# A two-layer hybrid decoder on one core: two weight fetches of layer 0's MLP moved ahead, its down groups reordered, and fewer down units threaded into the up

## The chip, the cores and the metric

The kernel runs on one core of a Trainium2 chip. The metric is the device time of one execution in microseconds (us), and of several executions the median. The engines are PE (TensorE, the matrix products), DVE (VectorE), ACT (ScalarE), POOL (GpSimd) and SP (SyncE, which here issues most DMAs); each works through its own instructions in order, and semaphores tie them together.

## The reference

All is float32, one sequence of 512 tokens, width 1024, MLP width 2816:

```python
def forward(x):
    h = x
    for i in range(2):
        hn = rms_norm(h, norm_mix[i])
        h = h + (pool_mixer(hn) if i == 0 else swa_sink_attention(hn))
        hn = rms_norm(h, norm_ffn[i])
        u = hn @ w_in                       # 1024 -> 2 * 2816
        c = causal_depthwise_conv3(u) + conv_b
        a, g = c[..., :2816], c[..., 2816:]
        h = h + (a * silu(g)) @ w_out       # 2816 -> 1024
    return rms_norm(h, norm_f)
```

The pool mixer takes causal means over windows of 2, 4, 8 and 16 tokens in four channel groups; the attention is a sliding window of 128 with 16 query heads, 4 key heads, sinks and ALiBi.

## The kernel before, in words

Activations lie with channels on the 128 partitions and tokens along the free axis; `h` is eight such tiles of 128 x 512. Every float32 product is made of three matmuls of rounded parts: each operand is split into a high part (`_h`, an ACT copy, line 101 or 427) and the rest (`_l`, a subtraction on DVE or POOL, line 104 or 428), and `mm3` (lines 87 to 89) issues high x high, high x low and low x high.

The change lies in layer 0's MLP, `mlp_halves`. The MLP width is cut into 22 blocks of 128 (j = 0 to 21), each with a gate part and a value part.

- **Blocks 0 to 6** are done as 14 plain chunks (gate and value, eight `mm3` each). Their weights are `wi`; the `_l` part of these is made on POOL in four pieces. After each chunk a short text in the table of line 537 says, by the chunk's number, which other steps are issued: `1` takes one finished chunk through norm, convolution and gating (a "late job" on DVE and ACT), `0` and `2` build the activation sums `th`/`tl`, `f` fetches a block's summed weights, `r` and `v` split them, `m` fetches and splits the first down weights.
- **Blocks 7 to 21** are each done with seven half-size products in place of eight, on sums of quarters of the weights and sums of token halves. A block has four weight tiles: `uw_u` (two sums, made by a plain DMA on SP and an accumulating DMA on POOL into the same tile), `uw_r` (two plain quarters), `uw_v` (made from `uw_r` and `uw_u` by two adds on POOL, in place in the `uw_r` tile, lines 450 and 451) and `uw_q` (one quarter). A product is twelve matmuls of 256 columns. In an iteration j of the loop the next block's weights are split (`first_weights`, `second_weights`) and those of the block after that fetched (`fetch_sums`).
- **The down product** of layer 0 runs inside this loop. Finished blocks `z` are taken in groups (`DOWN0` gives their sizes); for each group and each of the eight tiles of `h` (m = 0 to 7) one down weight `wo` is fetched, split and used: a group of four has four *units* per m, a unit being one `mm3` of 512 columns. `FILL` gives how many units an iteration j threads between its products, at four stops; what remains runs behind the loop. The last group also makes, for each m, the normalised input of the attention (`ax`, lines 240 and 241) and its square sums (lines 204 and 213).

Buffers come from rings: `wh`/`wl` of 4 serve `uw_r`, `uw_q`, `wi` and `wo` together; `vh`/`vl` of 3 serve `uw_u` and `uw_v`; `raw` of 3 holds fetched weights; `sq` of 2 holds a fetched down weight and also the squares. The finished blocks z4 to z18 lie in the ring of eight that also holds other activations, the first four and the last three in their own.

The order of instructions on each engine is set by a list scheduler: it takes the steps as the program writes them, with its own costs, and puts each engine's instructions in one order, which the chip then follows.

Of the kernel before, what the change touches and what calls it, by code (L numbers as in the profile page):

```python
# [19 lines left out]
F32 = mybir.dt.float32  # L20
F32R = mybir.dt.float32r
# [13 lines left out]
FF = 2816  # L35
NF = FF // P
GROUPS = ((4, True), (4, True), (3, False))
DOWN0 = (4, 4, 4, 4, 4, 2)
PLAIN = 7
SETS = ((2, 2), (2, 2))  # L40
HD = 64
# [19 lines left out]
def trunk(ctx: ExitStack, tc: tile.TileContext, x_tok, x_t, vecs, w_pool, w_kq, w_v, w_o, gain, w_in, w_half, w_down, w_end, w_tok, out):  # L61
# [18 lines left out]
    def bank(tag):  # L80
        rings[tag].append(rings[tag].pop(0))
        return banks[rings[tag][-1]]
# [13 lines left out]
    def weights(src, n, name, eng=None, raw=None, step=1024, pin=lambda ins: ins):  # L96

        raw = raw or fetch(src, n, name)
        h = wp.tile([P, 1024], F32R, tag="wh", name=f"{name}_h")
        l = wp.tile([P, 1024], F32R, tag="wl", name=f"{name}_l")  # L100
        pin(A.activation(h[:, :n], raw[:, :n], AF.Copy))  # L101
        for a in range(0, n, step):
            o = slice(a, min(a + step, n))
            (eng or V).tensor_tensor(l[:, o], raw[:, o], h[:, o].bitcast(F32), ALU.subtract)  # L104
        return h, l
# [253 lines left out]
    def mlp_halves(fp, xs, norm, ws0, after):  # L359
# [9 lines left out]
        def valued(j, ps):  # L369
            t = conv_sum(fp, ps, j, f"a{j}")  # L370
            V.tensor_tensor(t, t, gate.pop(j), ALU.mult)
            own = j < 4 or j >= NF - 3
            zh, zl = (
                fp.tile([P, S], F32R, tag=f"z{k}", name=f"z{j}{k}", bufs=4)
                if own
                else xp.tile([P, S], F32R, tag=f"x{k}", name=f"z{j}{k}")
                for k in "hl"
            )
            A.activation(zh, t, AF.Copy)
            V.tensor_tensor(zl, t, zh.bitcast(F32), ALU.subtract)  # L380
            z.append((zh, zl))
# [8 lines left out]
        def blocks(t):  # L390
            return t.rearrange("p (a b) -> p a b", a=2)
# [33 lines left out]
        def own_split(raw, name):  # L425
            x, y = (fp.tile([P, 1024], F32R, tag=f"v{k}", name=f"{name}_{k}", bufs=3) for k in "hl")
            A.activation(x, raw, AF.Copy)  # L427
            V.tensor_tensor(y, raw, x.bitcast(F32), ALU.subtract)  # L428
            return x, y

        raws, uw = {}, {}

        def fetch_sums(j):

            src = w_half[j - PLAIN]
            u = fp.tile([P, 1024], F32, tag="ur", name=f"uw{j}_u_raw", bufs=2)
            nc.sync.dma_start(blocks(u), src[:, 0:4:2, :])
            pin(G.dma_start(blocks(u), src[:, 2:4, :], accum_op=ALU.add))
            r = wp.tile([P, 1024], F32, tag="raw", name=f"uw{j}_r_raw", bufs=3)
            nc.sync.dma_start(blocks(r), src[:, 0:2, :])  # L440
            raws[j] = u, r

        def first_weights(j):

            n = 4 * P
            u, r = raws[j]
            q = wp.tile([P, 1024], F32, tag="raw", name=f"uw{j}_q_raw", bufs=3)
            nc.sync.dma_start(q[:, :n], w_half[j - PLAIN][:, 3, :])
            R = weights(None, 2 * n, f"uw{j}_r", raw=r)
            G.tensor_tensor(r[:, :n], r[:, :n], u[:, n:], ALU.add)  # L450
            G.tensor_tensor(r[:, n:], r[:, n:], r[:, :n], ALU.add)
            raws[j] = r, q
            uw[j] = R, own_split(u, f"uw{j}_u")

        def second_weights(j):

            r, q = raws.pop(j)
            uw[j] += own_split(r, f"uw{j}_v"), weights(None, 4 * P, f"uw{j}_q", raw=q)

        def product(out, w, b, t, start=True):  # L460
            for p in range(4):
# [66 lines left out]
        for at in range(2, len(todo)):  # L528
            w, ps, ahead = ahead, chunk(at), load(at + 1)
            for k in range(NC):  # L530
                if at == 3 and k == 0:
                    r = norm.stats(bank("aux"), root=True)
                if at == 3 and k == 5:
                    rb = norm.spread(bank("aux"), r)
                    signs = spread_signs()
                mm3(ps, part(w, k), xs[k], k == 0, k == NC - 1)
            for x in {3: "00", 4: "00", 5: "1", 6: "22", 7: "12", 8: "21", 9: "1f1", 10: "1", 11: "1r", 12: "1vf", 13: "1m1"}.get(at, ""):
                if x == "0":
                    first_part(len(th))
                elif x == "2":  # L540
                    second_part(len(tv))
                elif x == "1":
                    work()
                elif x == "f":
                    fetch_sums(PLAIN + fetched)
                    fetched += 1
                elif x == "r":
                    first_weights(PLAIN)
                elif x == "m":
                    down_fetch(0)  # L550
                    down_fetch(1)
                    down_split(0)
                else:
                    second_weights(PLAIN)

        FILL = dict(zip(range(PLAIN, NF), (11, 11, 10, 11, 11, 10, 8, 8, 8, 8, 8, 8, 8, 8, 8)))
        fills = down()

        def fill(j, i):
# [8 lines left out]
        for j in range(PLAIN, NF):  # L568
            R, U, W, Q = uw.pop(j)
            if j + 1 < NF:  # L570
                first_weights(j + 1)
            ba, bx = bank("ps"), bank("ps")
            s1, s2 = (fp.tile([P, HS], F32, tag="sn", name=f"sn{j}{i}", bufs=4) for i in range(2))
            s3 = sm.tile([P, S], F32, tag="sqa", name=f"sn{j}2", bufs=1)[:, lo]

            product(ba[:, lo], R, 0, 0)
            A.activation(s1, ba[:, lo], AF.Copy)  # L577
            if last:
                last()
            work()  # L580
            fill(j, 0)
            product(ba[:, lo], W, 0, 5, False)
            A.activation(s2, ba[:, lo], AF.Copy, scale=-1.0)
            if j + 1 < NF:
                second_weights(j + 1)
            if j + 2 < NF:
                fetch_sums(j + 2)
            product(bx[:, lo], R, 1, 1)
            fill(j, 1)
            work()  # L590
            product(ba[:, lo], U, 0, 3, False)
            A.activation(s3, ba[:, lo], AF.Copy)
            product(bx[:, hi], U, 1, 4)
            fill(j, 2)
            product(ba[:, lo], Q, 0, 6, False)
            V.tensor_tensor(ba[:, hi], bx[:, hi], s3, ALU.add)
            jobs.append((gated, j, ba))
            work()

            def last(j=j, bx=bx, W=W, s1=s1, s2=s2):  # L600
                product(bx[:, hi], W, 1, 2, False)
                V.tensor_tensor(bx[:, lo], bx[:, lo], s1, ALU.subtract)
                V.tensor_tensor(bx[:, hi], s2, bx[:, hi], ALU.subtract)
                jobs.append((valued, j, bx))

            fill(j, 3)
# [644 lines left out]
```

## Time and profile before

| what | us |
|---|---|
| median of three runs | 938.29 (937.98 to 939.18) |
| the profiled execution | 939.86 |
| its span, first to last instruction | 938.2 |
| PE busy | 902.0 (96%) |
| DVE busy | 702.8 (75%) |
| ACT busy | 482.4 (51%) |
| POOL busy | 248.8 (27%) |
| mean granted PE clock, of full speed | 0.981 |

Matmuls are pipelined, so the duration of one is longer than the distance to the next. In a row of the time line stand the start, the duration, the engine, the line of the program, the operation, output<-inputs with buffer numbers left out, the shape, and in brackets the idle time of the engine before it with what ended it. "PE bank L87 <- ACT wo_h L101" in the list of waits reads: the matmul of line 87 waited for the ACT copy of line 101 that makes `wo_h`.

### The profile page before, as it was taken

To read this page: it belongs to the slowest core of one execution; us is meant where nothing else is said; L and a number is where in the kernel's file an instruction comes from. 1 tells how busy PE (TensorE), PEld (TensorE's weight loads), DVE (VectorE), ACT (ScalarE), POOL (GpSimd) and SP (SyncE) were. 2 spreads that over 40 slices of the span, in tenths; PEclk is the share of its full clock that TensorE was granted. 3 is DMA by queue.
4 is the path that set the end of the run, shared out by engine and by line. 5 is a ranking of instruction groups with operands and counts; after the bars stand their busy time and mean duration, and the time that the engine had idled before them with its cause. 6 is when DMAs were issued, how large, how long until landed. Compare 5 with 4: busy or idle time off the path is not lost.

```text
span 938.2 us, 13044 instructions
## 1 busy us (share of the span) xinstructions
PE 902.0 (96%) x4812; PEld 774.6 (83%) x4812; DVE 702.8 (75%) x1116; ACT 482.4 (51%) x776; POOL 248.8 (27%) x319
## 2 busy tenths in 40 slices
PE   8999679999999999879999999999999999999996
PEld 8888469999999999649888988888888888888885
DVE  7899587868787876655688664498896788976744
ACT  7755345545555654344788643365443444443434
POOL 3856311312323220150766322000230001210004
PEclk9999869999999999989999999999999999999999
DMA  8433335555555533122211013316268322443302
GB/s 326 139 112 80 101 105 152 136 148 143 148 156 148 156 104 97 37 101 68 92 45 47 23 64 138 112 46 221 71 161 246 110 90 68 90 138 110 103 32 90
DMA packets 37120, 106.85 MB, mean 114 GB/s; under 512 B 3904, under 2 KB 4928, under 8 KB 37056
## 3 DMA queue, kind: packets, MB, share of 16 engines
q1 hardware_dynamic: 33744, 93.95, 30.3%
q0 software_dynamic: 3312, 12.06, 7.4%
q8 instruction: 38, 0.62, 0.3%
q14 instruction: 26, 0.21, 0.1%
HBM read 103.90 MB, written 2.10 MB: 113 GB/s over the span
## 4 chain that ended last, share of the span: by engine, by line
PE 84%; DVE 5%; ACT 4%; POOL 2%; issue 2%; DMA 2%; DVEq 0%; ACTq 0%; POOLq 0%
PE bank L87 27%; PE bank L89 27%; PE bank L88 26%; DMA uw_u_raw<-w_half 2%; POOL wi_l L104 2%; PE bank L1083 1%; PE bank L1111 1%; DVE n_acc L502 1%; PE bank L285 1%; ACT sc L1099 0%; ACT wi_h L101 0%; ACT px_h L240 0%; ACT h L329 0%; DMA xt<-x_tok 0%; PE bank L726 0%
## 5 line engine op out<-in xcount | busy, mean ns | idle before, releaser
L87 PE MATMUL bank<-f1x_h,wi_h 128*128 128x512 f32 x352 | 137.9, 392 | 0.0
L89 PE MATMUL bank<-f1x_h,wi_l 128*128 128x512 f32 x352 | 137.1, 389 | 0.0
L88 PE MATMUL bank<-f1x_l,wi_h 128*128 128x512 f32 x352 | 137.0, 389 | 0.0
L101 ACT ACTIVATE wi_h<-wi_raw 128x1024 fp32r<-128x1024 f32 x58 | 61.3, 1060 | 88.7 <-PE bank L88 72.6
L89 PEld LDWEIGHTS bank<-f1x_h,wi_l 128*128 128x128 f32 x352 | 66.1, 188 | 13.9
L88 PEld LDWEIGHTS bank<-f1x_l,wi_h 128*128 128x128 f32 x352 | 66.1, 188 | 13.6
L87 PEld LDWEIGHTS bank<-f1x_h,wi_h 128*128 128x128 f32 x352 | 66.1, 188 | 13.4
L104 DVE TENSOR_TENSOR wi_l<-wi_raw,wi_h 128x1024 fp32r<-128x1024 f32 x44 | 53.7, 1225 | 30.2 <-ACT wi_h L101 29.4
L450 POOL TENSOR_TENSOR uw_r_raw<-uw_r_raw,uw_u_raw 128x512 f32<-128x512 f32 x15 | 20.0, 1336 | 187.6 <-DVE uw_r_l L104 182.0
L101 ACT ACTIVATE wo_h<-wo_raw 128x512 fp32r<-128x512 f32 (+2 forms) x56 | 36.9, 660 | 57.5 <-PE bank L88 55.7
L104 POOL TENSOR_TENSOR wi_l<-wi_raw,wi_h 128x256 fp32r<-128x256 f32 x56 | 55.0, 1014 | 34.3 <-ACT wi_h L101 34.3
L615 DVE TENSOR_TENSOR c_u<-bank,n_rb 128x512 f32<-128x512 f32 x44 | 30.1, 687 | 23.3 <-PE bank L89 23.3
L89 PE MATMUL bank<-f0x_h,wi_l 128*128 128x512 f32 x112 | 43.7, 390 | 1.0 <-POOL wi_l L104 1.0
L213 POOL TENSOR_TENSOR n_acc<-n_acc,n_sq 128x512 f32<-128x512 f32 x14 | 20.7, 1479 | 89.6 <-DVE h L492 47.1
L88 PE MATMUL bank<-f0x_l,wi_h 128*128 128x512 f32 x112 | 43.6, 389 | 0.0
L87 PE MATMUL bank<-f0x_h,wi_h 128*128 128x512 f32 x112 | 43.2, 391 | 0.0
L492 DVE TENSOR_TENSOR h<-bank,h 128x512 f32<-128x512 f32 x48 | 32.9, 685 | 12.8 <-PE bank L89 12.5
L620 DVE SCALAR_TENSOR_TENSOR c_t<-c_u,vec,c_t 128x510 f32<-128x510 f32 x44 | 40.9, 932 | 1.2
L104 DVE TENSOR_TENSOR wo_l<-wo_raw,wo_h 128x512 fp32r<-128x512 f32 (+2 forms) x52 | 36.6, 704 | 4.0 <-ACT wo_h L101 2.6
L87 PE MATMUL bank<-th,uw_v_h 128*128 128x256 f32 x120 | 34.6, 288 | 4.2 <-ACT sn L577 4.2
L757 POOL TENSOR_TENSOR wt_a_raw<-wt_a_raw,wt_s_raw 128x1024 f32<-128x1024 f32 x4 | 11.3, 2836 | 101.6 <-DVE wt_a_l L104 101.6
L428 DVE TENSOR_TENSOR uw_v_l<-uw_r_raw,uw_v_h 128x1024 fp32r<-128x1024 f32 x15 | 18.5, 1232 | 25.3 <-ACT uw_v_h L427 25.3
(438 smaller groups left out, 2858.8 us busy)
## 6 DMA issues: line engine op xcount, KB each, us to landing
wi_raw<-w_in SPq DMA_DIRECT2D x58, 512.0 KB, 3.4
wo_raw<-w_down SPq DMA_DIRECT2D x40, 256.0 KB, 3.4
uw_u_raw<-w_half SPq DMA_DIRECT2D x15, 512.0 KB, 3.7
uw_r_raw<-w_half SPq DMA_DIRECT2D x15, 512.0 KB, 4.0
uw_u_raw<-w_half POOLq DMA_DIRECT2D x15, 512.0 KB, 6.5
wt_a_raw<-w_tok SPq DMA_DIRECT2D x12, 512.0 KB, 4.7
kq_raw<-w_kq SPq DMA_DIRECT2D x10, 512.0 KB, 3.3
wo_raw<-w_o SPq DMA_DIRECT2D x8, 512.0 KB, 3.3
```

The costliest lines, as they stand in the source:

```text
L87: T.matmul(ps, lhsT=wh, rhs=xh, start=start, stop=False, **kw)
L88: T.matmul(ps, lhsT=wh, rhs=xl, start=False, stop=False, **kw)
L89: T.matmul(ps, lhsT=wl, rhs=xh, start=False, stop=stop, **kw)
L101: pin(A.activation(h[:, :n], raw[:, :n], AF.Copy))
L104: (eng or V).tensor_tensor(l[:, o], raw[:, o], h[:, o].bitcast(F32), ALU.subtract)
L213: eng.tensor_tensor(self.acc[:, lo:hi], self.acc[:, lo:hi], sq[:, lo:hi], ALU.add)
L428: V.tensor_tensor(y, raw, x.bitcast(F32), ALU.subtract)
L450: G.tensor_tensor(r[:, :n], r[:, :n], u[:, n:], ALU.add)
L492: V.tensor_tensor(h[m], ps, h[m], ALU.add)
L615: V.tensor_tensor(u, ps, rb, ALU.mult)
L620: V.scalar_tensor_tensor(t[:, 2:], u[:, : S - 2], cw[0], t[:, 2:], ALU.mult, ALU.add)
L757: G.tensor_tensor(r[:, :n], r[:, :n], raws["s1", s][:, :n], ALU.add)
```

## The change

Five edits, all in `mlp_halves` and its constants:

1. The summed weights of blocks 7 and 8 (`fetch_sums`) are fetched together after chunk 8 (`ff`), in place of one after chunk 9 and one after chunk 12. The plain quarters `uw_r`, which were fetched in the same step, are a step of their own (`fetch_rows`, `g`), after chunk 9 and chunk 13.
2. Block 7's `uw_r` and `uw_q` go to other tiles: one of the `vl` ring and one of the `sq` ring in place of two of the `raw` ring.
3. POOL's two adds for `uw_v` are a step of their own (`add_weights`, `a`), after chunk 12 for block 7. One more late job is issued after the chunks (eleven in place of ten).
4. The down groups have 4, 4, 2, 4, 4, 4 blocks in place of 4, 4, 4, 4, 4, 2; the last four finished blocks get tiles of their own.
5. `FILL`: from block 10 on, 9, 8, 8 and then 7 units an iteration in place of 11, 11, 10 and then 8. In all 120 in place of 136; 56 in place of 40 run behind the loop.

```diff
@@ -35,7 +35,7 @@
 FF = 2816
 NF = FF // P
 GROUPS = ((4, True), (4, True), (3, False))
-DOWN0 = (4, 4, 4, 4, 4, 2)
+DOWN0 = (4, 4, 2, 4, 4, 4)
 PLAIN = 7
 SETS = ((2, 2), (2, 2))
 HD = 64
@@ -369,7 +369,7 @@
         def valued(j, ps):
             t = conv_sum(fp, ps, j, f"a{j}")
             V.tensor_tensor(t, t, gate.pop(j), ALU.mult)
-            own = j < 4 or j >= NF - 3
+            own = j < 4 or j >= NF - 4
             zh, zl = (
                 fp.tile([P, S], F32R, tag=f"z{k}", name=f"z{j}{k}", bufs=4)
                 if own
@@ -430,32 +430,45 @@

         raws, uw = {}, {}

+        us, rs = {}, {}
+
         def fetch_sums(j):

             src = w_half[j - PLAIN]
-            u = fp.tile([P, 1024], F32, tag="ur", name=f"uw{j}_u_raw", bufs=2)
+            u = us[j] = fp.tile([P, 1024], F32, tag="ur", name=f"uw{j}_u_raw", bufs=2)
             nc.sync.dma_start(blocks(u), src[:, 0:4:2, :])
             pin(G.dma_start(blocks(u), src[:, 2:4, :], accum_op=ALU.add))
-            r = wp.tile([P, 1024], F32, tag="raw", name=f"uw{j}_r_raw", bufs=3)
-            nc.sync.dma_start(blocks(r), src[:, 0:2, :])
-            raws[j] = u, r
+
+        def fetch_rows(j):
+
+            if j > PLAIN:
+                rs[j] = wp.tile([P, 1024], F32, tag="raw", name=f"uw{j}_r_raw", bufs=3)
+            else:
+                rs[j] = fp.tile([P, 1024], F32R, tag="vl", name=f"uw{j}_r_raw", bufs=3).bitcast(F32)
+            nc.sync.dma_start(blocks(rs[j]), w_half[j - PLAIN][:, 0:2, :])

         def first_weights(j):

             n = 4 * P
-            u, r = raws[j]
-            q = wp.tile([P, 1024], F32, tag="raw", name=f"uw{j}_q_raw", bufs=3)
+            u, r = us[j], rs[j]
+            if j > PLAIN:
+                q = wp.tile([P, 1024], F32, tag="raw", name=f"uw{j}_q_raw", bufs=3)
+            else:
+                q = sm.tile([P, S], F32, tag="sq", name=f"uw{j}_q_raw")
             nc.sync.dma_start(q[:, :n], w_half[j - PLAIN][:, 3, :])
-            R = weights(None, 2 * n, f"uw{j}_r", raw=r)
+            raws[j] = q
+            uw[j] = weights(None, 2 * n, f"uw{j}_r", raw=r), own_split(u, f"uw{j}_u")
+
+        def add_weights(j):
+
+            n = 4 * P
+            u, r = us.pop(j), rs[j]
             G.tensor_tensor(r[:, :n], r[:, :n], u[:, n:], ALU.add)
             G.tensor_tensor(r[:, n:], r[:, n:], r[:, :n], ALU.add)
-            raws[j] = r, q
-            uw[j] = R, own_split(u, f"uw{j}_u")

         def second_weights(j):

-            r, q = raws.pop(j)
-            uw[j] += own_split(r, f"uw{j}_v"), weights(None, 4 * P, f"uw{j}_q", raw=q)
+            uw[j] += own_split(rs.pop(j), f"uw{j}_v"), weights(None, 4 * P, f"uw{j}_q", raw=raws.pop(j))

         def product(out, w, b, t, start=True):
             for p in range(4):
@@ -534,7 +547,7 @@
                     rb = norm.spread(bank("aux"), r)
                     signs = spread_signs()
                 mm3(ps, part(w, k), xs[k], k == 0, k == NC - 1)
-            for x in {3: "00", 4: "00", 5: "1", 6: "22", 7: "12", 8: "21", 9: "1f1", 10: "1", 11: "1r", 12: "1vf", 13: "1m1"}.get(at, ""):
+            for x in {3: "00", 4: "00", 5: "1", 6: "22", 7: "12", 8: "21ff", 9: "1g1", 10: "1r", 11: "11", 12: "1av", 13: "g1m1"}.get(at, ""):
                 if x == "0":
                     first_part(len(th))
                 elif x == "2":
@@ -546,6 +559,10 @@
                     fetched += 1
                 elif x == "r":
                     first_weights(PLAIN)
+                elif x == "g":
+                    fetch_rows(PLAIN + (at > 12))
+                elif x == "a":
+                    add_weights(PLAIN)
                 elif x == "m":
                     down_fetch(0)
                     down_fetch(1)
@@ -553,7 +570,7 @@
                 else:
                     second_weights(PLAIN)

-        FILL = dict(zip(range(PLAIN, NF), (11, 11, 10, 11, 11, 10, 8, 8, 8, 8, 8, 8, 8, 8, 8)))
+        FILL = dict(zip(range(PLAIN, NF), (11, 11, 10, 9, 8, 8, 7, 7, 7, 7, 7, 7, 7, 7, 7)))
         fills = down()

         def fill(j, i):
@@ -569,6 +586,7 @@
             R, U, W, Q = uw.pop(j)
             if j + 1 < NF:
                 first_weights(j + 1)
+                add_weights(j + 1)
             ba, bx = bank("ps"), bank("ps")
             s1, s2 = (fp.tile([P, HS], F32, tag="sn", name=f"sn{j}{i}", bufs=4) for i in range(2))
             s3 = sm.tile([P, S], F32, tag="sqa", name=f"sn{j}2", bufs=1)[:, lo]
@@ -585,6 +603,7 @@
                 second_weights(j + 1)
             if j + 2 < NF:
                 fetch_sums(j + 2)
+                fetch_rows(j + 2)
             product(bx[:, lo], R, 1, 1)
             fill(j, 1)
             work()
```

POOL's order around the accumulating fetches. Before, with `wi0_5_1` the weights of chunk 10, and so on:

```order
L104 TENSOR_TENSOR wi0_4_0_l_811<-wi0_4_0_raw_808,wi0_4_0_h_810 128x256 x4
L104 TENSOR_TENSOR wi0_5_1_l_857<-wi0_5_1_raw_854,wi0_5_1_h_856 128x256 x4
L438 DMA uw7_u_raw_897<-w_half 128x1024
L104 TENSOR_TENSOR wi0_5_0_l_911<-wi0_5_0_raw_908,wi0_5_0_h_910 128x256 x4
L104 TENSOR_TENSOR wi0_6_1_l_954<-wi0_6_1_raw_951,wi0_6_1_h_953 128x256 x4
L450 TENSOR_TENSOR uw7_r_raw_900<-uw7_r_raw_900,uw7_u_raw_897 128x512
L451 TENSOR_TENSOR uw7_r_raw_900<-uw7_r_raw_900 128x512
L104 TENSOR_TENSOR wi0_6_0_l_1005<-wi0_6_0_raw_1002,wi0_6_0_h_1004 128x256 x4
L438 DMA uw8_u_raw_1053<-w_half 128x1024
```

And in the changed program:

```order
L104 TENSOR_TENSOR wi0_4_0_l_811<-wi0_4_0_raw_808,wi0_4_0_h_810 128x256 x4
L440 DMA uw7_u_raw_854<-w_half 128x1024
L440 DMA uw8_u_raw_857<-w_half 128x1024
L104 TENSOR_TENSOR wi0_5_1_l_863<-wi0_5_1_raw_860,wi0_5_1_h_862 128x256 x4
L104 TENSOR_TENSOR wi0_5_0_l_914<-wi0_5_0_raw_911,wi0_5_0_h_913 128x256 x4
L466 TENSOR_TENSOR uw7_r_raw_903<-uw7_r_raw_903,uw7_u_raw_854 128x512
L467 TENSOR_TENSOR uw7_r_raw_903<-uw7_r_raw_903 128x512
L104 TENSOR_TENSOR wi0_6_1_l_967<-wi0_6_1_raw_964,wi0_6_1_h_966 128x256 x4
L104 TENSOR_TENSOR wi0_6_0_l_1016<-wi0_6_0_raw_1013,wi0_6_0_h_1015 128x256 x4
```

Both accumulating fetches moved ahead of the splits of chunks 10 to 13, and the two adds for block 7 ahead of those of chunks 12 and 13. The plain DMAs into the same two tiles stand on SP at the same place in both programs, ahead of block 5's weights.

ACT's order where block 8's summed weights are split. Before:

```order
L427 ACTIVATE uw7_v_h_1045<-uw7_r_raw_900 128x1024
L354 ACTIVATE g4_t_1083<-bank2_72,vec_90 128x512
L379 ACTIVATE z3h_1041<-a3_t_1036 128x512
L427 ACTIVATE uw8_u_h_1114<-uw8_u_raw_1053 128x1024
L101 ACTIVATE uw7_q_h_1049<-uw7_q_raw_990 128x512
L354 ACTIVATE a4_t_1097<-bank3_73,vec_90 128x512
L367 ACTIVATE g4_t_1083<-g4_t_1083 128x512
L101 ACTIVATE wo0_0_h_1092<-wo0_0_raw_1088 128x512
```

In the changed program it stands before the last two plain chunks' weights:

```order
L427 ACTIVATE uw7_v_h_1054<-uw7_r_raw_903 128x1024
L427 ACTIVATE uw8_u_h_1118<-uw8_u_raw_857 128x1024
L367 ACTIVATE g2_t_906<-g2_t_906 128x512
L101 ACTIVATE wi0_6_1_h_966<-wi0_6_1_raw_964 128x1024
L379 ACTIVATE z2h_950<-a2_t_945 128x512
L354 ACTIVATE g3_t_998<-bank6_76,vec_90 128x512
L354 ACTIVATE a3_t_1004<-bank7_77,vec_90 128x512
L101 ACTIVATE wi0_6_0_h_1015<-wi0_6_0_raw_1013 128x1024
```

What stood behind it before (`uw7_q`, block 4's value part, the first down weight `wo0_0`) now follows the same late work without it.

In the up, ACT's order at the end of iteration 11 in the changed program, and PE's at the same place (`wo1_4` is the down weight of group 1, m = 4):

```order
L427 ACTIVATE uw12_v_h_1912<-uw12_r_raw_1750 128x1024
L101 ACTIVATE wo1_4_h_1944<-wo1_4_raw_1840 128x512
L101 ACTIVATE wo1_5_h_2006<-wo1_5_raw_1948 128x512
L354 ACTIVATE g11_t_1994<-bank4_74,vec_90 128x512
L595 ACTIVATE sn120_2024<-bank0_70 128x256
```

```order
L87 MATMUL bank4_74<-th3_665,uw11_q_h_1743 128x256
L88 MATMUL bank4_74<-tl3_666,uw11_q_h_1743 128x256
L89 MATMUL bank4_74<-th3_665,uw11_q_l_1744 128x256
L87 MATMUL bank3_73<-z7h_1408,wo1_3_h_1836 128x512
L88 MATMUL bank3_73<-z7l_1409,wo1_3_h_1836 128x512
L89 MATMUL bank3_73<-z7h_1408,wo1_3_l_1837 128x512
L87 MATMUL bank2_72<-z4h_1094,wo1_4_h_1944 128x512
L88 MATMUL bank2_72<-z4l_1095,wo1_4_h_1944 128x512
L87 MATMUL bank0_70<-th0_611,uw12_r_h_1844 128x256
L88 MATMUL bank0_70<-tl0_612,uw12_r_h_1844 128x256
L89 MATMUL bank2_72<-z4h_1094,wo1_4_l_1945 128x512
```

The down weight's split follows that of `uw12_v` on ACT, and PE uses it one unit behind the Q product of iteration 11. Where a new down weight begins in an iteration follows from `FILL` and `DOWN0`, so with 7 units it drifts from one iteration to the next; with 8 units and groups of four it was at the same two stops in each.

## The prediction

> **What bounds the kernel now.** I read the page's busy shares first, then what PE waited for, then the stages by windows, then the time line of the two stages in which PE stops.
>
> ```profile
> span 938.2 us, 13044 instructions
> PE 902.0 (96%) x4812; PEld 774.6 (83%) x4812; DVE 702.8 (75%) x1116; ACT 482.4 (51%) x776; POOL 248.8 (27%) x319
> ...
> PE bank L87 <- ACT wo_h L101: 12.4, 4, 8.4
> PE bank L87 <- ACT sn L577: 4.2, 1, 4.2
> PE bank L89 <- DVE wo_l L104: 3.5, 4, 2.1
> PE bank L89 <- POOL wi_l L104: 1.0, 1, 1.0
> ```
>
> PE sets the time, at 96%, so only what makes PE wait, or run at a lower clock, can be won. The waits are few: in total us, number of times, longest. The windows (PE, PEld, DVE, ACT, POOL busy; then the granted clock) say where they lie.
>
> ```profile
> 90.00:100.00 10.00, 10.00 (x46) 8.28 (x45) 10.00 (x15) 5.95 (x9) 4.30 (x3) 1.00 0.16 52
> ...
> 110.00:120.00 10.00, 1.22 (x2) 0.50 (x2) 4.62 (x7) 3.99 (x7) 0.00 (x0) 0.55 0.44 112
> 120.00:130.00 10.00, 5.33 (x19) 4.42 (x20) 9.74 (x15) 5.47 (x11) 3.28 (x3) 0.50 0.13 33
> 130.00:140.00 10.00, 10.00 (x64) 9.23 (x64) 6.14 (x10) 4.48 (x8) 0.46 (x1) 0.93 0.58 151
> 142.00:363.00 221.00, 221.00 (x1504) 204.74 (x1504) 174.86 (x237) 119.97 (x179) 52.88 (x38) 1.00 0.51 141
> 363.00:414.00 51.00, 41.67 (x189) 32.07 (x188) 32.02 (x52) 22.23 (x38) 13.10 (x26) 0.94 0.14 43
> ```
>
> Two holes: 110 to 131, where the clock also stands at one half (0.55, 0.50, then 0.93), and one after 363, with 9 us of PE missing. Between them, from 142 to 363, PE never stops and has the full clock: the change can only lose there.
>
> **The first hole**, in the time line:
>
> ```profile
> 76.81 1.03 POOL L438 DMA_DIRECT2D uw_u_raw<-w_half  x1
> ...
> 101.27 4.24 POOL L104 TENSOR_TENSOR wi_l<-wi_raw,wi_h 128x256 fp32r<-128x256 f32 x4
> 105.46 0.89 POOL L438 DMA_DIRECT2D uw_u_raw<-w_half  x1
> 108.36 0.28 PE L88 MATMUL bank<-tl,uw_r_h 128*128 128x256 f32 x1
> 108.48 0.28 PE L89 MATMUL bank<-th,uw_r_l 128*128 128x256 f32 x1
> 113.77 1.06 ACT L427 ACTIVATE uw_u_h<-uw_u_raw 128x1024 fp32r<-128x1024 f32 x1 [8.20 <-DMA uw_u_raw<-w_half]
> 115.38 0.69 DVE L104 TENSOR_TENSOR uw_q_l<-uw_q_raw,uw_q_h 128x512 fp32r<-128x512 f32 x1 [7.95 <-ACT uw_q_h L101]
> 117.11 0.80 PE L87 MATMUL bank<-z0h,wo_h 128*128 128x512 f32 x1 [8.35 <-ACT wo_h L101]
> 126.32 0.37 ACT L577 ACTIVATE sn<-bank 128x256 f32<-128x256 f32 x1
> 126.74 0.58 PE L87 MATMUL bank<-th,uw_v_h 128*128 128x256 f32 x1 [4.22 <-ACT sn L577]
> ```
>
> POOL issues the accumulating fetch of block 8's summed weights at 105.46, because four splits stand ahead of it in its queue. The data is there at 113.7. ACT stands before that tile's split for 8.20 us, and behind it in ACT's order are uw7_q, the late chunks and the first down weight; so DVE stops for 7.95 us and PE for 8.35. Then DVE is the limit: from 115.38 to 126 it works without a gap (9.74 of 10 in the window), and ACT copies the first bank (line 577) only at 126.32, behind that work. PE's waits there add to 8.35 + 2.1 (the longest for wo_l above) + 4.2 = 14.7 us.
>
> **Part A: the early fetch.** In the new order both accumulating fetches stand on POOL before block 5's splits. Their plain halves are issued on SP long before in both programs, so only POOL's place held them. The wait of ACT is gone if the transfer takes its usual time:
>
> ```profile
> uw_u_raw<-w_half POOLq DMA_DIRECT2D x15, 512.0 KB, 6.5
> ```
>
> That is 6.5 us at the median, 8.3 here. Block 7's own fetch was issued at 76.81, right behind block 5's first four splits; both now stand ahead of these, so before 76.81. Even one behind the other at 8.3 us each, the second is there by 93.4, and its split stands at 113.77 today. What then? DVE's work in the stretch is the same: the late chunks (one job fewer is left for the loop), the splits, z4 and z5. So I do not count the whole hole. Everything behind DVE's pause comes 7.95 us earlier: line 577 at 118.4 and PE's second start at 118.8 in place of 126.74. The wait for the first down weight shrinks to one or two us, the wait for line 577 stays at about 5. **A = -8.0 us.** Ends: -4 if half of the work merely stays ahead of line 577 (DVE has no pause then, but uw8_u's split and one more chunk now stand in the chunks' time), -10.5 if the clock does not fall, which is worth about 2.5 us (30 matmuls at about twice 0.12 to 0.23).
>
> On that last point the rows come first: PE's last matmul starts at 108.48, and 0.55 in the window to 120 means 1 us at full clock and 9 at half, so the clock fell at about 111, 2.2 us after PE stopped, and came back near 131.4. The Trainium skill ("TensorE: Matmul & The Clock Gate", Part 1: The HAM clock gate) says that the clock is halved after an idle window of about 3.4 us that runs free of the program. By it a pause of 5 us may or may not hold a whole window, and A would be -8 or -10.5; the trace of this case shows a shorter pause punished.
>
> **Cost on POOL.** Two issues (0.89 above) now stand ahead of block 5's splits, and the two adds for block 7 ahead of block 6's. PE waited 1.0 us for a wi_l already (the waits above). I take **+0.5 us**; ends 0 (the chunks have slack) and +3 (both in full).
>
> **Part B: fewer down units in the up.** A unit is three 512-wide matmuls, at the pitch of the rows below 0.69 us. 136 units were threaded into the up, now 120; those 16 are moved, not removed, so PE's work is the same. But each of iterations 10 to 20 now holds 7 to 9 units in place of 8 to 11, and the split chain of the weights stays as long as it is:
>
> ```profile
> 198.88 1.04 ACT L101 ACTIVATE uw_r_h<-uw_r_raw 128x1024 fp32r<-128x1024 f32 x1
> 200.57 1.22 DVE L104 TENSOR_TENSOR uw_r_l<-uw_r_raw,uw_r_h 128x1024 fp32r<-128x1024 f32 x1
> 201.88 1.28 POOL L450 TENSOR_TENSOR uw_r_raw<-uw_r_raw,uw_u_raw 128x512 f32<-128x512 f32 x1 [17.07 <-DVE uw_r_l L104]
> 203.24 1.74 POOL L451 TENSOR_TENSOR uw_r_raw<-uw_r_raw 128x512 f32<-128x512 f32 x1
> 207.17 1.06 ACT L427 ACTIVATE uw_v_h<-uw_r_raw 128x1024 fp32r<-128x1024 f32 x1 [0.71 <-PE bank L88]
> 208.26 1.23 DVE L428 TENSOR_TENSOR uw_v_l<-uw_r_raw,uw_v_h 128x1024 fp32r<-128x1024 f32 x1 [0.94 <-ACT uw_v_h L427]
> 210.73 0.43 DVE L596 TENSOR_TENSOR bank<-bank,sn 128x256 f32<-128x256 f32 x1 [1.24 <-PE bank L89]
> 211.27 0.69 DVE L104 TENSOR_TENSOR wo_l<-wo_raw,wo_h 128x512 fp32r<-128x512 f32 x1
> ```
>
> In iteration 11, with 11 units, POOL's adds for block 12 end at 204.98 and the split uw_v_h waits for PE until 207.17: a slack of 2.2 us. With 8 units PE is 3 x 0.69 = 2.1 us sooner, and the slack is gone. Behind uw_v_h on ACT now stands the split of the next down weight, and on DVE its lower part stands behind uw_v_l and the sum of line 596: 1.06 + 1.23 + 0.43 + 0.69 = 3.4 us from the start of uw_v_h. PE has to do meanwhile one Q product (12 x 0.12 = 1.4 us), none to two units, and the weight's own first two matmuls (0.5 us): 1.9 to 3.3 us. So each down weight first used right behind a Q product can hold PE by 0.1 to 1.5 us, and up to 2.5 where the adds are late too. Before, that place is met by three down blocks from iteration 10 on, all in iterations of 10 or 11 units, and with 8 units a block always starts at the first or third stop. In the new order 7 + 1 drift: eight blocks meet it (group 1's 2, 4 and 6, group 2's 2 and 6, group 3's 1 and 6, group 4's 0). At 1.0 us each **B = +8 us**; ends +1 (0.1 each) and +20 (2.5 each).
>
> **Part C: the tail.** After the last product of the up:
>
> ```profile
> 366.18 0.40 PE L87 MATMUL bank<-z16h,wo_h 128*128 128x512 f32 x1
> 366.41 0.40 PE L88 MATMUL bank<-z16l,wo_h 128*128 128x512 f32 x1
> ...
> 371.82 0.40 PE L87 MATMUL bank<-z16h,wo_h 128*128 128x512 f32 x1
> 396.55 0.50 PE L87 MATMUL bank<-z20h,wo_h 128*128 128x512 f32 x1 [2.79 <-ACT wo_h L101]
> 399.10 0.42 ACT L101 ACTIVATE wo_h<-wo_raw 128x256 fp32r<-128x256 f32 x1 [0.63 <-DMA wo_raw<-w_down]
> 399.98 0.69 DVE L492 TENSOR_TENSOR h<-bank,h 128x512 f32<-128x512 f32 x1 [2.17 <-PE bank L89]
> 407.69 0.69 DVE L492 TENSOR_TENSOR h<-bank,h 128x512 f32<-128x512 f32 x1 [0.34 <-PE bank L89]
> 412.99 0.80 PE L89 MATMUL bank<-ax_h,kq_l 128*128 128x512 f32 x1 [3.22 <-DVE kq_l L104]
> 425.49 0.72 PE L219 MATMUL bank<-ones,n_acc 128*128 128x2 f32 x6
> ```
>
> From 371.82 to 425.49 PE does 40 units and the first two key projections: 120 + 48 matmuls at 0.23 = 38.6 us of work in 53.7 us. So 15.0 us are lost. The last group had two units a block: 6 x 0.23 = 1.4 us of PE against a pace of (407.69 - 399.98) / 3 = 2.6 us that fetch, split, residual add, normalised copy and square allow. Now the last group has four units a block, 2.8 us: PE is slower than that pace, and the key weights' split finds DVE free. The blocks' fetch is 256 KB in place of 128, and their splits grow by 0.2 us on ACT and 0.3 on DVE, so the pace becomes about 3.1: some 0.3 us stay lost at each of eight blocks, 2.5 in all. **C = -12.5 us**; ends -15 (nothing stays) and -7 (1 us a block).
>
> **Sum:** -8.0 + 0.5 + 8 - 12.5 = -12.0. The profiled execution has 939.86 us, 1.7 of it outside its span of 938.2; it becomes 927.9. It lies 1.6 above the median of the runs shown, 938.29, so the median becomes **926.3**.
>
> **Rivals.**
>
> 1. The start is bound by DVE's backlog more than I think: DVE is busy 10.00 of 10 us from 90 to 100, and the work moved ahead only delays blocks 5 and 6. A is -4, POOL's cost +2; the sum -6.5, **931.8**. Against it: the 7.95 us pause is real idle time.
> 2. The up does not notice the thinner filling (B = +1), since DVE is busy only 174.86 of 221 us there. The sum is -19, **919.3**. Against it: the slack of 2.2 us is all used up by 2.1.
> 3. Slower: the chain through POOL's adds becomes the pace of the up. If uw_v_h is late in each of the eleven iterations 10 to 20, by 2.2 us, B is +24 and the sum +4, **942.3**. It decides from about 1.8 us an iteration (20 / 11). For it: the chain from 198.88 to 204.98 is fixed, 6.1 us, and starts only when PE frees a buffer; against it: in the 8-unit iterations of before PE never stops.
> 4. The change does not do what it says: POOL or SP could still hold the fetch. The order shows POOL's issues four splits earlier; 938 again.
>
> **Chances.** The forecast 0.66; rival 1 0.14; rival 2 0.13; rival 3 0.05; rival 4 0.02. My range is 920.5 to 932.5: it holds the forecast with its smaller errors (922 to 930) and most of rival 1, and ends short of rival 2's middle. A measurement here can tell about 0.2% from no change, 1.9 us. Faster by more than that: 0.92; within it 0.03; slower 0.05.
>
> **What would show it.** A: the row of uw_u_h for block 8 without a DMA wait, no pause of 8 us on DVE near 107 to 115, and PE's wait for line 577's successor still there, 4 to 6 us. B: waits of PE for wo_h and wo_l between 200 and 350, about eight places of about 1 us; none at all is rival 2, one in every iteration rival 3. C: no wait for kq_l of 3.2 us, and no lower clock in the tail (0.94 in the window above). The forecast is wrong if the first hole stays over 15 us, or if PE's waits between 142 and 363 add to less than 3 or more than 15.

## The result and the profile after

The changed kernel takes **927.36 us** (median of 4 runs, 926.32 to 928.19) beside 938.73 for the kernel before (4 runs, 937.98 to 939.99). The ratio is 0.9877, with a 95% interval of 0.986 to 0.9894. The forecast was 926.3, in a range of 920.5 to 932.5. The profiled execution went from 939.86 to 926.93 us, 12.9 less (forecast: 12.0 less).

Page of the changed kernel, then its list of PE's waits (total us, times, longest):

```profile
span 925.2 us, 13037 instructions
PE 900.2 (97%) x4812; PEld 772.1 (83%) x4812; DVE 702.9 (76%) x1116; ACT 478.9 (52%) x776; POOL 247.1 (27%) x319
...
PE bank L89 <- DVE wo_l L104: 5.9, 8, 1.1
PE bank L87 <- ACT sn L595: 4.3, 2, 4.0
PE bank L87 <- DVE g_t L356: 3.5, 1, 3.5
```

Of the 12.4 us for wo_h 0.2 are left, and the 1.0 for wi_l is gone. The 4 us for the successor of line 577 (now 595) have stayed. The waits for wo_l have grown from 3.5 to 5.9, and a wait of 3.5 us for a bank that `g_t` frees is new. The windows (same columns as in the prediction) say where:

```profile
110.00:120.00 10.00, 6.05 (x35) 5.21 (x33) 9.75 (x14) 5.15 (x8) 0.38 (x1) 0.93 0.14 50
120.00:130.00 10.00, 10.00 (x61) 9.25 (x61) 7.74 (x12) 5.70 (x10) 3.87 (x3) 0.90 0.64 155
...
142.00:350.00 208.00, 203.31 (x1391) 186.10 (x1390) 163.73 (x227) 109.57 (x171) 49.74 (x37) 1.00 0.52 142
350.00:404.00 54.00, 51.89 (x244) 41.59 (x243) 34.82 (x50) 23.48 (x37) 9.22 (x11) 1.00 0.23 69
```

The hole of 110 to 131 has become a short one, with the clock at 0.93 and 0.90 in place of 0.55 and 0.50. The up now has idle time of PE (203.31 of 208 us), where the kernel before had none. Behind it 2.1 us are idle, not 9.3, and the clock stays whole.

Three marks of the program divide the gain. The first product of block 8's R weight starts at 142.29 before and 133.22 after, so the start gave **-9.1 us**. The last matmul of the up starts at 371.70 and 359.35, 12.35 earlier. 9.1 of it came from the start, and 48 matmuls of the down (16 units) fewer stand ahead, 11.0 us at 0.23. So the up lost **+7.8 us**. From there to the first sum of line 219 (425.49 and 412.58) the trace shows 53.8 us and 53.2 us, for 168 and 216 matmuls of 0.23 each. The time lost is 15.1 before and 3.5 after, **-11.6 us**. The sum is -12.9.

### The profile page after: what moved, and what is told of

It reads as the page before. It is cut to its first block, busy times and chain, and to the rows that moved or that the text cites. A ratio compares the mean times of both kernels' runs of the same rounds, so it can differ in the third digit from the quotient of the medians.

```text
span 925.2 us, 13037 instructions
## 1 busy us (share of the span) xinstructions
PE 900.2 (97%) x4812; PEld 772.1 (83%) x4812; DVE 702.9 (76%) x1116; ACT 478.9 (52%) x776; POOL 247.1 (27%) x319
## 4 chain that ended last, share of the span: by engine, by line
PE 66%; DVE 3%; ACT 2%; DMA 2%; issue 1%; POOL 1%; ACTq 0%; DVEq 0%; SPq 0%; POOLq 0%
PE bank L89 21%; PE bank L87 21%; PE bank L88 21%; PE bank L1102 1%; PE bank L1130 1%; DMA uw_u_raw<-w_half 1%; DMA wo_raw<-w_down 1%; DVE wo_l L104 1%; ACT sc L1118 1%; DVE uw_u_l L428 0%; ACT wo_h L101 0%; PE bank L745 0%; DVE h L505 0%; DVE uw_r_l L104 0%; ACT uw_u_h L427 0%
## 5 line engine op out<-in xcount | busy, mean ns | idle before, releaser
L466 POOL TENSOR_TENSOR uw_r_raw<-uw_r_raw,uw_u_raw 128x512 f32<-128x512 f32 x15 | 22.0, 1464 | 179.5 <-DVE uw_r_l L104 173.2
L776 POOL TENSOR_TENSOR wt_a_raw<-wt_a_raw,wt_s_raw 128x1024 f32<-128x1024 f32 x4 | 11.3, 2834 | 103.3 <-DVE wt_a_l L104 103.3
L637 ACT ACTIVATE c_t<-c_u,vec 128x512 f32<-128x512 f32 x44 | 35.3, 806 | 2.8 <-DVE c_u L634 2.6
```

The lines of the kernel that those rows point to most:

```text
L637: A.activation(t, u, AF.Identity, bias=col(V_CB + layer * 2 * NF + m), scale=cw[2])
L776: G.tensor_tensor(r[:, :n], r[:, :n], raws["s1", s][:, :n], ALU.add)
```

## The experiments

In the texts on record, "iteration 11" is the pass of the up loop for block 11. The times of the kernel before beside the runs were 939.21 us (e1 to e4), 939.43 (e5 to e8) and 938.66 (e9, e10).

### What the units of the up cost: e1, e2, e3

The prediction blamed the up's loss on thin iterations and on the place behind a Q product. The trace of the changed kernel suggested another reason. These are rows from iteration 11 (PE's last ones of the second R product, then the chain that follows), and below them the first splits of the R weights in other iterations:

```profile
191.41 0.28 PE L88 MATMUL bank<-tl,uw_r_h 128*128 128x256 f32 x1
191.74 1.06 ACT L101 ACTIVATE uw_r_h<-uw_r_raw 128x1024 fp32r<-128x1024 f32 x1 [0.94 <-PE bank L88]
194.47 1.67 POOL L466 TENSOR_TENSOR uw_r_raw<-uw_r_raw,uw_u_raw 128x512 f32<-128x512 f32 x1 [18.74 <-DVE uw_r_l L104]
196.21 1.62 POOL L467 TENSOR_TENSOR uw_r_raw<-uw_r_raw 128x512 f32<-128x512 f32 x1
197.86 1.06 ACT L427 ACTIVATE uw_v_h<-uw_r_raw 128x1024 fp32r<-128x1024 f32 x1 [2.80 <-POOL uw_r_raw L467]
200.43 0.68 DVE L104 TENSOR_TENSOR wo_l<-wo_raw,wo_h 128x512 fp32r<-128x512 f32 x1
201.16 0.50 PE L89 MATMUL bank<-z4h,wo_l 128*128 128x512 f32 x1 [0.68 <-DVE wo_l L104]
...
208.47 1.06 ACT L101 ACTIVATE uw_r_h<-uw_r_raw 128x1024 fp32r<-128x1024 f32 x1 [0.94 <-PE bank L88]
224.62 1.06 ACT L101 ACTIVATE uw_r_h<-uw_r_raw 128x1024 fp32r<-128x1024 f32 x1 [0.94 <-PE bank L88]
288.80 1.06 ACT L101 ACTIVATE uw_r_h<-uw_r_raw 128x1024 fp32r<-128x1024 f32 x1 [0.94 <-PE bank L88]
297.97 1.05 ACT L101 ACTIVATE uw_r_h<-uw_r_raw 128x1024 fp32r<-128x1024 f32 x1
333.60 1.07 ACT L101 ACTIVATE uw_r_h<-uw_r_raw 128x1024 fp32r<-128x1024 f32 x1 [0.94 <-PE bank L88]
```

The split of block 12's R weight starts when PE has read block 11's R weight for the last time (191.41 + 0.28 = 191.69). The ring of four, which R, Q and down weights share, gave it that buffer. It is so in five iterations (11, 12, 13, 17 and 20), 1.3 us ahead of the first U product; where the buffer came from a down weight, as at 297.97, the split stands 4 to 8 us ahead. What follows it is then late too: POOL's two adds, the split of V on ACT, which waits 2.80 us for POOL, the down weight's split behind that on ACT and DVE, and PE. PE waits right behind this chain in three of the five iterations (at 201.16, 217.99 and 343.04), 2.6 us in all above the usual pitch. The other waits of the up above 0.2 us, 3.4 us by the same count, lie between 241 and 276, around the group with two units a down weight:

```profile
241.89 0.50 PE L89 MATMUL bank<-z8h,wo_l 128*128 128x512 f32 x1 [1.13 <-DVE wo_l L104]
...
266.80 0.42 ACT L101 ACTIVATE wo_h<-wo_raw 128x256 fp32r<-128x256 f32 x1 [4.13 <-DMA wo_raw<-w_down]
...
275.51 0.50 PE L89 MATMUL bank<-z10h,wo_l 128*128 128x512 f32 x1 [0.74 <-DVE wo_l L104]
```

The R splits ahead of these (234.15, 254.01 and 267.78) are not late; ACT stands 4.13 us for the fetch of one of that group's down weights. What sets each of these waits was not tested.

Which buffer the ring gives depends on how many down weights have taken one by then, so the running count of units decides, and not only how many an iteration holds. Three runs with 120 units each, as in the changed kernel, tell this apart:

```diff
-FILL: (11, 11, 10, 9, 8, 8, 7, 7, 7, 7, 7, 7, 7, 7, 7)
+e1:   (8, 8, 8, 8, 8, 8, 8, 8, 8, 8, 8, 8, 8, 8, 8)
+e2:   (10, 8, 8, 8, 8, 8, 8, 8, 8, 8, 8, 8, 8, 8, 6)
+e3:   (9, 8, 8, 8, 8, 8, 8, 8, 8, 8, 8, 8, 8, 8, 7)
```

> The changed kernel with eight down units in every iteration of the up (120 in all, as in the changed kernel, which has 11, 11, 10, 9, 8, 8 and then 7). Buffer theory: in iterations 11, 12, 13, 17 and 20 of the changed kernel the split of the next block's R weight starts only when PE has ended the second R product of the block itself (1.3 us ahead of the first U product, where it stands 4 to 8 us ahead in the others), because it gets the buffer of the R weight before it; the up loses 7.7 us in all. With eight units and blocks that begin at the first or third stop no such wait arises: 927.4 - 7.7 = 919.7 us, and no wait of PE between 142 and 350 over 0.5 us. Place theory (the prediction's part B: a down block first used behind a Q product waits): none is met except in group 2, whose two-unit blocks begin at every stop: 920 to 922. Thin-filling theory (fewer than eight units leave PE short): 919.7, or later by up to 3 us if iterations 7 to 9 now run short with 8 in place of 11.

> The changed kernel with 10 units in iteration 7, eight in 8 to 20 and 6 in 21 (120 in all): every iteration but two is as full as in the run with eight everywhere, but the blocks of four begin at the second and the fourth stop, so in each iteration one is first used right behind the Q product. Place theory: that place is met some ten times more than with eight everywhere, 1.0 us each: about 930. Buffer theory: the R weight's split gets the buffer of a down weight whose last unit is done well before the second R product, so no wait: 919.7, within 1 us of the run with eight everywhere. Thin-filling theory: 919.7 too.

> The changed kernel with 9 units in iteration 7, eight in 8 to 20 and 7 in 21 (120 in all): one unit off the run with eight everywhere. Buffer theory: now the R weight's split gets the buffer of the R weight before it in eleven iterations, and of a late down weight in two; the changed kernel lost 7.7 us by five such iterations, 1.5 us each, so this one loses about 17: 919.7 + 17 = 936.5 us, with PE's waits for wo_h and wo_l in nearly every iteration from 8 to 20. Place theory: a block begins one unit behind the Q product, 0.7 us later than in the run that begins right behind it: 0.3 us each at most, 923. Thin-filling theory: eight units in every iteration, 919.7.

Measured: e1 **918.85 us** (918.76 to 919.35; ratio to before 0.9786, 0.9773 to 0.98), e2 **920.76** (0.9808, 0.9795 to 0.9821), e3 **935.45** (0.9964, 0.9952 to 0.9977). PE's waits in e1, in e2 and in e3, and of e3 one late split with what follows:

```profile
PE bank L89 <- DVE wo_l L104: 2.0, 3, 0.7
```

```profile
PE bank L89 <- DVE wo_l L104: 1.8, 3, 0.7
PE bank L87 <- ACT wo_h L101: 1.4, 2, 1.2
```

```profile
PE bank L89 <- DVE wo_l L104: 9.9, 15, 1.0
PE bank L87 <- ACT wo_h L101: 2.0, 2, 1.4
...
139.37 1.06 ACT L101 ACTIVATE uw_r_h<-uw_r_raw 128x1024 fp32r<-128x1024 f32 x1 [0.94 <-PE bank L88]
145.49 1.06 ACT L427 ACTIVATE uw_v_h<-uw_r_raw 128x1024 fp32r<-128x1024 f32 x1 [2.80 <-POOL uw_r_raw L467]
148.79 0.50 PE L89 MATMUL bank<-z0h,wo_l 128*128 128x512 f32 x1 [0.69 <-DVE wo_l L104]
165.53 0.50 PE L89 MATMUL bank<-z0h,wo_l 128*128 128x512 f32 x1 [0.69 <-DVE wo_l L104]
```

e2 and e3 hold the same number of units in all but the first and the last iteration, and differ by one unit of offset; the time differs by 14.7 us, and e3 differs from e1 by 16.6 (the buffer theory said 17). In e3 the R split waits for PE 11 times (9.5 us in all), and an iteration takes 165.53 - 148.79 = 16.74 us in place of 15.6; eleven times the difference is 12.5 of the 16.6 us, and most of the rest lies again around the group with two units. The addresses that the programs give their tiles agree with the buffer theory: the high part of the next block's R weight lies where the current block's lies in iterations 11, 12, 13, 17 and 20 of the changed kernel, in eleven iterations of e3 (8 to 14 and 17 to 20), and in none of the up loop in e1, e2 and the kernel before. In e1 and e2 PE's only long wait in the up is one of 1.2 us in e2, for the first block behind the two-unit group. The place theory fails by e2: a block is first used right behind the Q product in nearly every iteration, and PE does not wait there, as in these rows:

```profile
184.17 1.05 ACT L101 ACTIVATE uw_r_h<-uw_r_raw 128x1024 fp32r<-128x1024 f32 x1
191.02 1.06 ACT L427 ACTIVATE uw_v_h<-uw_r_raw 128x1024 fp32r<-128x1024 f32 x1 [1.00 <-PE bank L88]
193.58 0.28 PE L89 MATMUL bank<-th,uw_q_l 128*128 128x256 f32 x1
193.70 0.40 PE L87 MATMUL bank<-z4h,wo_h 128*128 128x512 f32 x1
```

The thin-filling theory fails by e3: eight units in every iteration but two, and it loses 16.6 us against e1, where the changed kernel loses 8.5.

### The new wait at the start: e4

The wait of 3.5 us that nothing in the prediction foresaw, in the changed kernel:

```profile
73.08 1.95 POOL L440 DMA_DIRECT2D uw_u_raw<-w_half  x2
...
82.44 1.06 ACT L427 ACTIVATE uw_u_h<-uw_u_raw 128x1024 fp32r<-128x1024 f32 x1 [1.80 <-DMA uw_u_raw<-w_half]
...
84.36 0.76 ACT L354 ACTIVATE g_t<-bank,vec 128x512 f32<-128x512 f32 x1
87.83 0.66 PE L87 MATMUL bank<-f0x_h,wi_h 128*128 128x512 f32 x1 [3.52 <-DVE g_t L356]
```

Block 7's U split now stands ahead of the last `th` and of the late chunks on ACT. In the kernel before it stood behind them, and `g_t` of that chunk began at 79.42, not 84.36. It waits for the accumulating fetch, 9.3 us after its issue. The edit:

```diff
-7: "12",   8: "21ff", 9: "1g1"
+7: "12ff", 8: "21",   9: "1g1"
```

> The changed kernel with the fetches of both summed weights one chunk sooner in the program (behind chunk 7's steps in place of chunk 8's), so that POOL issues both accumulating fetches ahead of four more splits, in a stretch where it stands idle for 5.5 us. Fetch theory: the new wait of PE near 84 us (3.5 us, for a bank that a late chunk's g_t frees) comes from ACT standing 1.8 us for block 7's accumulating fetch, ahead of th and of the late chunks, and from the four splits that POOL does 2 us later; both go, and the first R product starts 3.5 to 4 us earlier: 923.4 to 924. Backlog theory: DVE is behind by then in any case and the wait stays: 927.4. In between: the 1.8 us alone, 925.6.

Measured: **925.1 us** (923.14 to 925.95; ratio 0.9848, 0.9833 to 0.9863), 2.3 less than the changed kernel, nearest to the case in between, though not for the reason given there. Rows of e4:

```profile
63.35 1.96 POOL L440 DMA_DIRECT2D uw_u_raw<-w_half  x2
...
85.58 0.47 PE L87 MATMUL bank<-f0x_h,wi_h 128*128 128x512 f32 x1 [0.54 <-DVE g_t L356]
110.77 0.50 PE L89 MATMUL bank<-z0h,wo_l 128*128 128x512 f32 x1 [0.86 <-DVE wo_l L104]
116.00 0.58 PE L87 MATMUL bank<-th,uw_v_h 128*128 128x256 f32 x1 [4.03 <-ACT sn L595]
```

The fetch theory is right on its place: the wait is down to 0.54 us, and the first R product starts at 107.42 in place of 111.31. But of these 3.9 us only 2.2 arrive at the second weight's product (118.24 to 116.00). A wait of 0.86 us for the first wo_l came back, and the copy of line 595 is late by the same 4 us. So something behind the first R product also limits the second start of PE.

### The parts alone: e5, e6, e7

e5 is the kernel before with the fetch, the rows and the tiles of the change; e6 is the kernel before with the other lines of the diff; e7 is e1 with the old groups:

```diff
 e6:
-DOWN0 = (4, 4, 4, 4, 4, 2)
+DOWN0 = (4, 4, 2, 4, 4, 4)
-own = j < 4 or j >= NF - 3
+own = j < 4 or j >= NF - 4
-FILL = ... (11, 11, 10, 11, 11, 10, 8, 8, 8, 8, 8, 8, 8, 8, 8)
+FILL = ... (11, 11, 10, 9, 8, 8, 7, 7, 7, 7, 7, 7, 7, 7, 7)
```

> The kernel before with the early fetch alone: the groups of the down are 4, 4, 4, 4, 4, 2 and the units of the up 11, 11, 10, 11, 11, 10 and then 8, as before. In the two traces the second part of block 7 starts 8.5 us sooner in the changed kernel (126.74 to 118.24) and block 8 9.1 us sooner (142.29 to 133.22). If the parts add, this run gains those 9.1 us and nothing else: 938.7 - 9.1 = 929.6 us, with no wait of PE for a down weight in the up and 15 us lost behind it, as before. If the waits of the up came from the new place of the fetches or of the blocks' tiles, they stand here too: 937.

> The kernel before with the new groups of the down (4, 4, 2, 4, 4, 4) and the new numbers of units in the up, and the fetch where it was. If the parts add: 938.7 + 7.7 (the up's waits) - 11.6 (behind the up, 15.15 us lost in the kernel before and 3.5 in the changed one) = 934.8 us, with the first hole of 21 us as before, and the R weight's split late in iterations 11, 12, 13, 17 and 20. Buffer theory and parts that add agree on this. If the waits of the up need the early fetch: 927.

> The run with eight units everywhere, but with the groups of the down as in the kernel before (4, 4, 4, 4, 4, 2): the same 120 units in the up and the same 56 behind it, of which the last 16 are two a block. Pace theory (the prediction's part C: two units a block are shorter than the pace of fetch, split, residual add and normalised copy, and the key weights' split comes late behind it): the 15.15 us lost behind the up come back in place of 3.5: 918.9 + 11.6 = 930.5. If the gain is only that more units stand behind the up, 919 to 921.

Measured: e5 **930.67 us** (ratio 0.9912, 0.9898 to 0.9926), e6 **936.31** (0.9965, 0.9952 to 0.9978), e7 **930.15** (0.99, 0.9886 to 0.9914). Against the kernel before beside them e5 gains 8.8 us and e6 3.1; the sum, 11.9, agrees with the whole change's 11.4. So the parts add. The waits of the up need no early fetch: in e5 PE is busy 208.00 of 208 us from 142 to 350, and in e6 the R split waits 0.94 us for PE in the same five iterations. e7 has the 120 units of e1 in the up and as many behind it, and loses what e1 does not:

```profile
386.62 0.50 PE L87 MATMUL bank<-z20h,wo_h 128*128 128x512 f32 x1 [2.78 <-ACT wo_h L101]
...
402.63 0.80 PE L89 MATMUL bank<-ax_h,kq_l 128*128 128x512 f32 x1 [3.20 <-DVE kq_l L104]
```

That is 11.3 us against e1. So the gain behind the up comes from the order of the groups (the last group has four units a down weight), and not from the number of units there.

### Both improvements: e8

> The two improvements together: eight units in every iteration (-8.5 us in its run against the changed kernel) and both fetches one chunk sooner (-2.3 us). They lie in different stretches: 918.85 - 2.3 = 916.6 us. If DVE's backlog at the start eats more of the second with eight units in iteration 7 in place of 11: 917.5 to 918.9.

Measured: **916.48 us** (915.71 to 917.04; ratio to before 0.9758, 0.9745 to 0.9772). It beats both kernels, the changed one by 10.9 us, and the two gains add to within 0.2 us. The wait that stays at the start is the longest that is left behind the first 10 us of work:

```profile
PE bank L87 <- ACT sn L595: 4.0, 1, 4.0
```

### The last wait at the start: e9, e10

What holds ACT's copy of line 595? If it is DVE's amount of work, a split less on DVE brings it forward. e9 leaves out the low part of block 7's second weight (its products take the U weight's low part), e10 does that split on POOL:

```diff
 e9:  uw[7] += (uw7_v_h, uw7_u_l), ...
 e10: for a in range(0, 1024, 256):
          G.tensor_tensor(y[:, a:a+256], raw[:, a:a+256], x[:, a:a+256], ALU.subtract)
```

> The run with both improvements, without the split of block 7's second weight into its low part on DVE (1.76 us there, at 100.98); the products of that weight take the low part of the U weight in its place, so this low part is left out of the computation. In that run PE waits 4.2 us, from 111 to 115.4, for ACT's copy of the first bank (line 595), which stands behind two late chunks that wait for DVE. Backlog theory (DVE's work ahead of 115 sets the second start of PE): 1.2 to 1.8 us sooner, 914.7 to 915.3. Order theory (the place of the copy in ACT's order sets it: the order made anew puts other late work in the gap): 916.5, or later by up to 1.5.

> The run with both improvements, with the same split on POOL in four pieces of 256 (POOL stands idle for 15.1 us from 101.7) in place of DVE. Backlog theory: 914.7 to 915.3, less what DVE's operations with two operands from SBUF lose beside POOL (371 took 0.80 and 428 1.76 beside POOL in that run, 0.68 and 1.21 without): 915 to 916. Order theory: 916.5 or later.

Measured: e9 **917.87 us** (0.9777, 0.9764 to 0.9791), e10 **918.04** (0.9778, 0.9765 to 0.9792). Neither is faster than e8; by the medians they are 1.4 and 1.6 us slower. The 914.7 to 915.3 us of the backlog theory are out of reach, so it is refuted in the form that it had. In e9 (line 598 is the copy):

```profile
114.44 0.62 ACT L379 ACTIVATE z5h<-a_t 128x512 fp32r<-128x512 f32 x1
115.53 0.78 ACT L354 ACTIVATE a_t<-bank,vec 128x512 f32<-128x512 f32 x1 [0.47 <-DVE bank L384]
116.20 0.37 ACT L598 ACTIVATE sn<-bank 128x256 f32<-128x256 f32 x1
```

With a split less the order was made anew, and `z5h` and one more late chunk now stand ahead of the copy; in e8 they stood behind it, and the copy ran at 114.95. So the late work that stands ahead of the copy in ACT's order, and waits for DVE, sets this wait in these runs; DVE's work is still part of it, since in e8 too ACT stands 1.89 us for DVE (at 112.12) ahead of the copy. A kernel with the copy further ahead was not run, so whether that would gain the 4 us stays open.

## Why the prediction was right, point by point

**The sum** was -12.0 and came to -12.9 in the profiled executions, and to -11.4 in the medians. Each part came near its forecast: A with POOL's cost -7.5 against -9.1, B +8 against +7.8, C -12.5 against -11.6. e5 and e6 confirm A and the sum of B and C by runs of their own (-8.8 and -3.1). No rival came true: A was not halved (rival 1, 931.8), the up did notice (rival 2, 919.3), and the late chain did not stand in every iteration (rival 3, 942.3). e3 shows that rival 3 was near: one unit of offset puts the chain in eleven iterations, and the time is then 16.6 us above that of e1.

**Part A, the hole.** Right: block 8's U split has no wait, DVE's pause is gone, PE's second start was forecast for 118.8 and is at 118.24, and the wait for line 577's successor stayed (3.95 us). Wrong: the first down weight has no wait at all, where one or two us were forecast, but for a reason outside that step, since the first R product itself came 4.15 us later (107.16 to 111.31). With that delay gone (e4), the wait is there: 0.86 us. The forecast was also closer than its reasons: in e4 block 8's first product stands 1.7 us further ahead (131.51 in place of 133.22), so without the new wait A would have come to about -10.8 us, beyond its end of -10.5. A gain that was set too low and a loss that was not foreseen cancel in part, which is luck.

**Cost on POOL**, the step that failed in its mechanism. The prediction asked what POOL's two issues do to the splits behind them (+0.5). It had not asked what stands behind the *data*: the step "its split stands at 113.77 today" looked at block 8 only. Block 7's U split moved ahead of `th` and the late chunks on ACT, the fetch took 9.3 us, beside another, where 8.3 was assumed, and PE lost 3.5 us for a bank. It cost little in the end (2.3 us by e4), since the stretch behind was bound by other work anyway.

**The clock.** The prediction held that a pause of about 5 us would still be punished, and took -8 rather than -10.5. The clock did fall at both pauses, but it came back after 3.4 us each time (the last section).

**Part B, right in size and in the chain, wrong in its cause.** The chain ahead of a late down weight is the one quoted: V's split on ACT, the down weight's upper half behind it, V's low part, a sum, the down weight's low part. The failed step is "With 8 units PE is 2.1 us sooner, and the slack is gone". In e1 and e2 all iterations, or all but two, have 8 units, and in the up PE does not wait for a down weight beyond the one wait of 1.2 us in e2, so that step does not hold. Where the slack is gone, the chain *starts* late, from a buffer of the ring that PE frees with its second R product. The prediction had the thought among its rivals ("starts only when PE frees a buffer") and did not follow it. So its eight places were mostly wrong. Three of them waited (the down weights 4 and 6 of group 1 and 0 of group 4: at 201.16, 217.99 and 343.04), and two others did (weight 1 of group 2 and weight 0 of group 3, 1.3 us each above the usual pitch), which do not follow a late R split directly. That 1 us at eight places and the true 7.8 us agree is largely chance. About 1.8 of the 7.8 us lie in pieces of less than 0.2 us.

**Part C.** Right: no wait for kq_l and no lower clock in the tail. What stays lost is 3.5 us, not 2.5: three waits for a last-group wo_l, of 0.5 to 0.73 us, and the rest in pieces of about 0.3 us or less. e7 shows by itself that the order of the groups does it.

## What to carry to other kernels

A count that threads work into a loop also sets which buffer of a shared ring the next step gets. Here one unit of offset was worth 15 to 17 us with the amount of work unchanged, so before a loop is blamed for being too thin or too full, look at what the *first* late instruction of the chain waited for, and try the same total at another phase. A fetch that is moved ahead moves its consumer in the other engines' orders too: ask what stands behind that consumer, if the data is late by a few us.

## What the hardware showed that was not expected

**The half clock comes in whole windows of about 3.4 us.** The last column but two is the granted clock (2 us a row). In the changed kernel, around its two pauses (PE stops at 84.3 and 114.3, and starts again at 87.83 and 118.24):

```profile
86.00:88.00 2.00, 0.17 (x1) 0.20 (x2) 2.00 (x4) 0.95 (x2) 1.19 (x2) 0.98 0.00 0
88.00:90.00 2.00, 2.00 (x6) 1.51 (x5) 2.00 (x4) 2.00 (x4) 2.00 (x3) 0.50 0.00 0
90.00:92.00 2.00, 2.00 (x7) 1.59 (x6) 2.00 (x4) 1.21 (x3) 0.78 (x2) 0.66 0.47 143
...
118.00:120.00 2.00, 1.76 (x10) 1.76 (x10) 2.00 (x3) 0.19 (x1) 0.38 (x1) 0.66 0.00 0
...
122.00:124.00 2.00, 2.00 (x13) 1.78 (x13) 1.30 (x2) 1.10 (x2) 1.95 (x2) 0.98 0.66 202
```

If such a row mixes a full clock (1.00) with a half one (0.50), the edge lies inside: 0.98 is 1.92 us at full, so the clock fell at 87.92; 0.66 is 0.64 us at full, so it came back at 91.36. It was low from 87.92 to 91.36 and from 118.64 to 122.08, 3.44 us each. By the same reading it was low for 6.8 us in e8 (112.56 to 119.36) and for 20.48 us in the kernel before (110.96 to 131.44): one, two and six times 3.41 us. The two falls of the changed kernel lie 30.72 us apart, nine times 3.41. So the clock does not follow a pause at once: it fell 3.6 and 4.3 us after PE had stopped here, 2.2 in the kernel before and 1.2 in e8, as the edges of the windows lay. The Trainium skill ("TensorE: Matmul & The Clock Gate", Part 1: The HAM clock gate) states such a window of about 3.4 us, running free of the program, and the trace agrees on both. On one point the runs differ from it. It calls for an idle window, and in e8 the window that ended at 112.56 was not idle: PE stopped at 111.35 and had worked for some 1.3 of its 3.4 us. Where PE had worked for about 2.5 of 3.4 us (111.8 to 115.2 in the changed kernel) the clock stayed.

For the prediction's question (-8 or -10.5) this means that in these runs a pause of 4 us is punished by one or two low windows, as their edges lie. In the changed kernel PE works 3.4 us at half speed behind each pause, about 1.7 us lost; in e8 it works from 115.38 to 119.36 so, 2.0 us lost.
